# Tiles of u split whole, attention output's weights split a tile ahead, dummy matmuls at the start: one step of a hybrid RG-LRU / attention / PEER block

## The chip, the cores and the metric

One core of one Trainium2 chip runs the whole program. The metric is the device time of one launch in microseconds, the median of several executions. The engines are TensorE (PE, with its weight loads as PEld), VectorE (DVE), ScalarE (ACT), GpSimd (POOL) and SyncE (SP), which here only issues DMAs.

## The reference, cut to what matters

A block over 512 tokens plus 16 meta tokens, width 1024, all float32. A gated recurrent branch and an attention branch are mixed into h. Then comes a product-key expert layer (PEER) over 16384 experts, and a last norm:

```python
n1 = _rmsnorm(h, norm1_g[l])
xr, gr, cq, ckv, kr, g_rnn, g_att = jnp.split(n1 @ w_in[l], IN_SPLITS, axis=-1)
...
y_att = o @ w_attn_out[l]
mixed = jax.nn.sigmoid(g_rnn) * y_rnn + jax.nn.sigmoid(g_att) * y_att
h = h + mixed @ w_out[l]
h = h + _peer(_rmsnorm(h, norm2_g[l]), ...)
...
# _peer, per block of 128 tokens
s1, s2 = q1 @ keys1.T, q2 @ keys2.T          # 8 heads, 128 keys each
t1, i1 = lax.top_k(s1, 16);  t2, i2 = lax.top_k(s2, 16)
ts, sel = lax.top_k(t1 + t2 (all pairs), 16);  idx = the chosen experts
act = jax.nn.gelu(jnp.einsum('chkd,cd->chk', u[idx], xt))
coef = softmax(ts) * act
return jnp.einsum('chk,chkd->cd', coef, v[idx])
```

## The kernel before, in words

Every large product is made of three matmuls of fp32r operands (`mm3`): each operand is split into a high part, a rounding copy made on ACT, and a low part, what is left, made by a subtraction on DVE (`split`, L154 to L156). PE takes high by high, low by high and high by low (L181 to L183). The weights of the dense layers come tile by tile through `wload` (L160 to L173): a tile of 1024 by 128 is loaded as two halves of 128x512 by two DMAs on SP, and each half has its own cast and its own subtraction. The raw halves, the high and the low parts each have a ring of three buffers in the pool "wstream".

The work runs in this order. **Start**: the columns of x and the first weights are loaded, the norm's gain is split into n1h and n1l, squares are taken on ACT (L263) and added on DVE (L265), and PE makes the latents' products (`wckv`) and then the sum of squares `n_ss` over partitions. Then come the projections, the recurrence and the attention. **Mixing** (`mixing`, L672): for each of eight column tiles m, the output weights of attention (`watt`) are split, PE makes `ya`, and the tile is mixed. **Key scores** (`key_scores`, L724): 16 tiles of the query weights `wq`, the scores against the keys, and the two best-eight passes of DVE over each row.

**PEER.** Three of the four blocks of 128 tokens (named 1, 2, 3 in the order of `ORDER`) are computed densely: for each of 128 tiles j of experts, PE makes `a` = u tile times the tokens (24 matmuls of 384 columns), ACT takes its gelu, DVE multiplies it by a gate matrix `gt`, and PE makes `y` = v tile times that (18 matmuls of 512 columns). Block 0 is computed by gathers of its chosen rows of u and v on POOL's queue (`first_by_index` L926, `second_by_index` L935) with multiply-adds on DVE. The gate matrices of the dense blocks are made ahead in a **scatter stage** (`scatter`, L843 to L894): for each group of eight heads' columns DVE builds one-hot matrices `hb` (128x1024, bf16) and `hot` (128x1024, fp32), ACT scales `wj`, PE multiplies them into `sc`, ACT copies `stg`, a DMA stores them to DRAM (`gd`). While that runs, PE makes the first 44 tiles of `a` (`first_ahead`, L830), and DVE also makes the choice of the best pairs (`choose`, L757 to L815: rounds of best-eight, then products over 256 to 1600 columns, L803 to L806). The **dense stage** then runs tile a(j+41) and y(j) in turn.

The tiles of u (`ut`) go through `wload` as well. Up to the dense stage a scheduler sets each engine's order; in the dense stage the order is that of the program. **Tail** (L993 to L1011): for each block of tokens two adds of y on DVE, squares and a square root on ACT, a reciprocal on DVE, and two multiplications (L1010) on DVE, each followed by a DMA on SP.

## Time and profile before

| | before |
|---|---|
| time, median of 3 runs | 1863.86 us (1862.81 to 1864.69) |
| the profiled execution: its own time | 1864.08 us |
| the profiled execution: span from first to last instruction | 1862.3 us, granted clock 0.994 |
| PE busy | 1811.8 us, 97% |
| DVE busy | 1444.0 us, 78% |
| ACT busy | 968.5 us, 52% |
| POOL busy | 355.2 us, 19% |

The span lies 1.8 us below the execution's own time, and the execution 0.2 us above the median of the runs. Busy shares are averages over stages with different limits: the dense stage alone lasts from about 960 to 1853 us.

### The profile page before, as it was taken

How to read it: one execution, taken by the hardware profiler on the slowest of the kernel's cores; microseconds unless marked ns; L12 is line 12 of the kernel's file. 1: busy time of each engine (PE TensorE's matmuls, PEld its weight loads, DVE VectorE, ACT ScalarE, POOL GpSimd, SP SyncE). 2: the span in 40 equal slices, each digit the busy share in tenths (PEclk: the TensorE clock that was granted, in tenths of full speed). 3: DMA queues.
4: the chain of work that ended last, by engine and by line, in shares of the span. 5: the costliest groups of instructions: out<-in, count | busy, mean ns of one | idle time of the engine just before them, and what ended most of it. 6: DMA issues, size and time to landing. Idle time of an engine off the chain costs nothing.

```text
span 1862.3 us, 28323 instructions
## 1 busy us (share of the span) xinstructions
PE 1811.8 (97%) x9731; PEld 1601.3 (86%) x9731; DVE 1444.0 (78%) x3088; ACT 968.5 (52%) x2011; POOL 355.2 (19%) x295
## 2 busy tenths in 40 slices
PE   8999999999899999999999999999999999999997
PEld 7888778877778889998999999999999999997886
DVE  7787677777546999997558788877888878887775
ACT  6778576766333337999953333433333333333343
POOL 0100000000100000000014344434444443543310
PEclk9999999999999999999999999999999999999999
DMA  5333212112743223445589999998998989988764
GB/s 163 96 98 105 74 55 66 57 60 75 237 131 125 80 85 125 177 164 193 191 295 336 324 322 352 318 315 307 321 332 310 322 310 322 333 300 272 266 219 153
DMA packets 181600, 390.32 MB, mean 210 GB/s; under 512 B 16593, under 2 KB 68305, under 8 KB 179921
## 3 DMA queue, kind: packets, MB, share of 16 engines
q1 hardware_dynamic: 141632, 245.97, 39.0%
q0 software_dynamic: 39536, 142.00, 22.1%
q8 instruction: 76, 1.25, 0.3%
q10 hardware_dynamic: 288, 0.56, 0.1%
q14 instruction: 68, 0.55, 0.1%
HBM read 353.44 MB, written 34.08 MB: 208 GB/s over the span
## 4 chain that ended last, share of the span: by engine, by line
PE 30%; issue 16%; POOL 6%; DMA 5%; DVE 4%; ACT 1%; DVEq 0%; POOLq 0%; ACTq 0%
PE y L183 5%; PE y L181 5%; PE y L182 5%; PE a L183 4%; POOL v L915 4%; PE a L181 4%; PE a L182 4%; PE sc L869 4%; DMA v<-in_peer_v_dram,eidx 3%; POOL u L915 2%; DMA u<-in_peer_u_dram,eidx 1%; DVE hot L884 1%; DMA gt<-gd 1%; DMA ut_w<-in_peer_uT_dram 0%; DVE ut_l L156 0%
## 5 line engine op out<-in xcount | busy, mean ns | idle before, releaser
L183 PE MATMUL a<-xdh,ut_l 128*128 128x384 f32 x1024 | 347.4, 339 | 9.2 <-DVE ut_l L156 9.2
L181 PE MATMUL a<-xdh,ut_h 128*128 128x384 f32 x1024 | 348.6, 340 | 1.7 <-ACT ut_h L155 1.4
L182 PE MATMUL a<-xdl,ut_h 128*128 128x384 f32 x1024 | 345.5, 337 | 0.3 <-DVE xdl L156 0.3
L155 ACT CAST ut_h<-ut_w 128x512 fp32r<-128x512 f32 x256 | 157.8, 624 | 327.2 <-DMA ut_w<-in_peer_uT_dram 277.9
L181 PE MATMUL y<-vh,ch 128*128 128x512 f32 x768 | 299.6, 390 | 5.4 <-ACT ch L155 5.4
L183 PE MATMUL y<-vh,cl 128*128 128x512 f32 x768 | 301.6, 393 | 0.0
L182 PE MATMUL y<-vl,ch 128*128 128x512 f32 x768 | 301.0, 392 | 0.0
L915 POOL DMA_INDIRECT u<-in_peer_u_dram,eidx x128 | 161.4, 1261 | 666.3 <-DMA gt<-gd 441.4
L915 POOL DMA_INDIRECT v<-in_peer_v_dram,eidx x128 | 175.4, 1370 | 266.8 <-DVE acc L935 239.7
L156 DVE TENSOR_TENSOR ut_l<-ut_w,ut_h 128x512 fp32r<-128x512 f32 x256 | 169.5, 686 | 54.5 <-ACT ut_h L155 51.3
L183 PEld LDWEIGHTS a<-xdh,ut_l 128*128 128x128 f32 x1024 | 194.1, 190 | 11.4 <-DVE ut_l L156 11.0
L181 PEld LDWEIGHTS a<-xdh,ut_h 128*128 128x128 f32 x1024 | 194.3, 190 | 6.1 <-ACT ut_h L155 2.3
L182 PEld LDWEIGHTS a<-xdl,ut_h 128*128 128x128 f32 x1024 | 194.1, 190 | 3.9 <-DVE xdl L156 0.5
L156 DVE TENSOR_TENSOR vl<-vr,vh 128x1024 fp32r<-128x1024 f32 x128 | 157.6, 1232 | 42.9 <-ACT vh L155 41.9
L155 ACT CAST ch<-gt 128x384 fp32r<-128x384 f32 x128 | 65.7, 513 | 232.4 <-DVE gt L965 227.7
L181 PEld LDWEIGHTS y<-vh,ch 128*128 128x128 f32 x768 | 144.7, 188 | 34.8 <-ACT ch L155 6.5
L935 DVE SCALAR_TENSOR_TENSOR acc<-v,coef,acc 128x1024 f32<-128x1024 f32 x128 | 164.1, 1282 | 10.5 <-DMA v<-in_peer_v_dram,eidx 8.5
L183 PEld LDWEIGHTS y<-vh,cl 128*128 128x128 f32 x768 | 144.4, 188 | 31.1 <-DVE cl L156 0.8
L182 PEld LDWEIGHTS y<-vl,ch 128*128 128x128 f32 x768 | 144.5, 188 | 28.5
L926 DVE SCALAR_TENSOR_TENSOR jk<-u,xn 128x1024 bf16<-128x1024 f32 x128 | 156.6, 1223 | 13.7 <-DMA u<-in_peer_u_dram,eidx 11.3
L155 ACT CAST vh<-vr 128x1024 fp32r<-128x1024 f32 x128 | 133.8, 1045 | 32.5 <-PE y L183 28.5
L156 DVE TENSOR_TENSOR cl<-gt,ch 128x384 fp32r<-128x384 f32 x128 | 71.5, 559 | 81.8 <-ACT ch L155 81.8
(348 smaller groups left out, 3470.2 us busy)
## 6 DMA issues: line engine op xcount, KB each, us to landing
ut_w<-in_peer_uT_dram SPq DMA_DIRECT2D x256, 256.0 KB, 6.1
vr<-in_peer_v_dram SPq DMA_DIRECT2D x128, 512.0 KB, 6.7
...
```

What stands on the lines that cost most here:

```text
L155: A.copy(dst_hi, src)
L156: V.tensor_sub(dst_lo, src, r32(dst_hi))
L181: TE.matmul(o, lh, rh, start=first, stop=False)
L182: TE.matmul(o, lh, rl, start=False, stop=False)
L183: TE.matmul(o, ll, rh, start=False, stop=last)
L869: TE.matmul(o[:, u * P:(u + 1) * P], hot[:, h + u, :], wj[:, h + u, :], start=True, stop=True)
L884: V.tensor_tensor(hot, iota.unsqueeze(1).to_broadcast([P, SG, P]), it[:, t0:t0 + SG].unsqueeze(2).to_broadcast([P, SG, P]), op=OP.is_equal)
L915: G.indirect_dma_start(out=t, out_offset=None, in_=src, in_offset=bass.IndirectOffsetOnAxis(ap=eidx[:, s:s + 1], axis=0))
L926: V.scalar_tensor_tensor(jk, t, 1.0, xn2, op0=OP.mult, op1=OP.mult, accum_out=coef[:, s:s + 1])
L935: V.scalar_tensor_tensor(acc, t, coef[:, s:s + 1], acc, op0=OP.mult, op1=OP.add)
```

## The change: whole tiles of u, weights of mixing ahead, dummy matmuls, and a tail on three engines

1. **u.** From tile 1 on, a tile of u is loaded by one DMA of 128x1024, and has one cast and one subtraction of 128x1024 (`uparts`). Tile 1 goes through the ring of v (`vr`, `vh`, `vl`), earlier than before; the others have rings of two whole tiles in a pool "ustream", which is opened where the weights' pool is closed, after the key scores. The pool "choice" moves to the other side of the memory.
2. **Mixing.** The load and split of watt for tile m+1 stand before the mixing of tile m.
3. **Start.** Ten matmuls of a 128x128 matrix of ones stand ahead of all others; ACT runs in program order there, which puts the squares behind the casts; the loads are written into the same loop.
4. **Tail.** For the first dense block (`fo1`) ACT scales by the reciprocal and POOL multiplies by the gain, instead of DVE.

```diff
+WARM = 10
-WB, RB, GB, VB, XB = 3, 3, 4, 3, 1
+WB, RB, GB, VB = 3, 3, 4, 3
...
-    wp = pool(ctx, "wstream")
+    wpx = ExitStack()
+    ctx.enter_context(wpx)
+    wp = pool(wpx, "wstream")
...
-        i = k * m
-        hi, lo = w[i // 512]
-        return hi[:, i % 512:i % 512 + m], lo[:, i % 512:i % 512 + m]
+        i, n = k * m, w[0][0].shape[-1]
+        hi, lo = w[i // n]
+        return hi[:, i % n:i % n + m], lo[:, i % n:i % n + m]
...
-    for k in range(NK):
-        nc.sync.dma_start(h0[k], hT[:, k * T:(k + 1) * T])
-        if k == 0:
-            w0 = wload(win[3], D, "wckv0")
     V.memset(onesP, 1.0)
     V.memset(eps_t, EPS)
-    A.activation(one_t, onesP[:, 0:1], AF.Identity)
-    for k in range(NK):
-        gk = vec[:, V_G1 + k:V_G1 + k + 1]
-        A.activation(n1h[:, k, :], h0[k], AF.Identity, scale=gk)
-        V.scalar_tensor_tensor(n1l[:, k, :], h0[k], gk, r32(n1h)[:, k, :], op0=OP.mult, op1=OP.subtract)
-    lat = [now(proj_tile(3 + k, True, f"wckv{k}", w=None if k else w0)) for k in range(2)]
-    sq = two(("cv", "aa"), "sq")
-    for k in range(NK):
-        A.activation(sq[k], h0[k], AF.Square)
-        if k:
-            V.tensor_add(sq[0], sq[0], sq[k])
+    warm = mm1("warm")
+    for _ in range(WARM):
+        TE.matmul(warm[:, :P], onesP, onesP, start=True, stop=True)
+    with in_order(tc, mybir.EngineType.Activation):
+        A.activation(one_t, onesP[:, 0:1], AF.Identity)
+        for k in range(NK):
+            nc.sync.dma_start(h0[k], hT[:, k * T:(k + 1) * T])
+            gk = vec[:, V_G1 + k:V_G1 + k + 1]
+            A.activation(n1h[:, k, :], h0[k], AF.Identity, scale=gk)
+            V.scalar_tensor_tensor(n1l[:, k, :], h0[k], gk, r32(n1h)[:, k, :], op0=OP.mult, op1=OP.subtract)
+            if k == 0:
+                w0 = wload(win[3], D, "wckv0")
+        lat = [now(proj_tile(3 + k, True, f"wckv{k}", w=None if k else w0)) for k in range(2)]
+        sq = two(("cv", "aa"), "sq")
+        for k in range(NK):
+            A.activation(sq[k], h0[k], AF.Square)
+            if k:
+                V.tensor_add(sq[0], sq[0], sq[k])
...
-            w = wload(peer_uT[j], D, f"ut{j}")
+            w = uload(j) if j else wload(peer_uT[j], D, f"ut{j}")
...
+        nw = wload(watt[0], D, "watt0")
         for m in range(NK):
-            w = wload(watt[m], D, f"watt{m}")
+            w = nw
...
             o = mm2(f"ya{m}")
             for k in range(NK):
                 mm3(o, *wsl(w, k), *ot[k], k == 0, k == NK - 1)
+            if m + 1 < NK:
+                nw = wload(watt[m + 1], D, f"watt{m + 1}")
...
-    po_ = pool(postx, "choice")
+    po_ = pool(postx, "choice", "right")
...
+    def uparts(j, pl, tags, bufs):
+
+        raw, hi, lo = (pl.tile([P, D], dt, tag=t, bufs=n, name=f"ut{j}_{t}")
+                       for t, n, dt in zip(tags, bufs, (F32, F32R, F32R)))
+        nc.sync.dma_start(raw, peer_uT[j])
+        split(hi, lo, raw)
+        return [(hi, lo)]
+
+    def uload(j):
+        return uparts(j, up, ("uw", "uh", "ul"), (2, 2, 2))
...
+            if m == 2 * PH - 1:
+                nextw[1] = uparts(1, vp, ("vr", "vh", "vl"), (VB, 2, 2))
             if m:
                 scores(m - 1, last)
             last = q2
-            if m == 2 * PH - 1:
-                nextw[1] = wload(peer_uT[1], D, "ut1")
...
-            w = nextw.pop(j, None) or wload(peer_uT[j], D, f"ut{j}")
+            w = nextw.pop(j, None) or uload(j)
             if j + 1 <= LAG - LT:
-                nextw[j + 1] = wload(peer_uT[j + 1], D, f"ut{j + 1}")
+                nextw[j + 1] = uload(j + 1)
...
     interleave((key_scores(), 17), (ga[0], na_[0]))
+    wpx.close()
+    up = pool(dx, "ustream")
...
-    wn[:] = 0, XB, vq
...
-        w = wload(peer_uT[j + LAG], D, f"ut{j + LAG}") if j + LAG < NJ else None
+        w = uload(j + LAG) if j + LAG < NJ else None
...
-            V.scalar_tensor_tensor(fo[:, cs], y[:, cs], st[:, 2:3], gfb[:, cs], op0=OP.mult, op1=OP.mult)
+            if i == 0:
+                A.activation(fo[:, cs], y[:, cs], AF.Copy, scale=st[:, 2:3])
+                G.tensor_mul(fo[:, cs], fo[:, cs], gfb[:, cs])
+            else:
+                V.scalar_tensor_tensor(fo[:, cs], y[:, cs], st[:, 2:3], gfb[:, cs], op0=OP.mult, op1=OP.mult)
```

The scheduler orders the engines anew after this. Three places of the new order follow; names carry the program's numbers, and line numbers of the changed kernel are its own (there L158 and L159 are the cast and the subtraction of a split).

DVE in the scatter stage, before, around the low part of tile 24 of u (`ut24_l`); `hb1`, `hot1` are the one-hot matrices of block 1, and `work0`, `oh0`, `efx0` the last steps of the choice for block 0:

```order
L803 TENSOR_TENSOR work0_9438<-sf0_10079,cand_pos_6197 128x640
L805 TENSOR_TENSOR oh0_1_10161<-work0_9438,cx0_9441 128x32x20
L884 TENSOR_TENSOR hot1_80_9118<-iota_73,it1_8523 128x1024
L879 TENSOR_TENSOR hb1_88_9147<-iota4_6199,blk1_8521 128x1024
L156 TENSOR_TENSOR ut24_l0_9068<-ut24_w0_9065,ut24_h0_9067 128x512
L156 TENSOR_TENSOR ut24_l512_9074<-ut24_w512_9071,ut24_h512_9073 128x512
L884 TENSOR_TENSOR hot1_88_9149<-iota_73,it1_8523 128x1024
L806 TENSOR_REDUCE efx0_80<-oh0_1_10161 128x8x4
L879 TENSOR_TENSOR hb1_96_9216<-iota4_6199,blk1_8521 128x1024
L803 TENSOR_TENSOR work0_9438<-sf0_10079,cand_pos_6197 128x1120
L805 TENSOR_TENSOR oh0_2_10244<-work0_9438,cx0_9441 128x32x35
L806 TENSOR_REDUCE efx0_80<-oh0_2_10244 128x8x4
```

The same place of the changed kernel:

```order
L826 TENSOR_REDUCE efx0_80<-oh0_1_9960 128x8x4
L899 TENSOR_TENSOR hb1_72_8929<-iota4_6210,blk1_8434 128x1024
L823 TENSOR_TENSOR work0_9291<-sf0_9884,cand_pos_6208 128x1120
L825 TENSOR_TENSOR oh0_2_10037<-work0_9291,cx0_9294 128x32x35
L904 TENSOR_TENSOR hot1_72_8931<-iota_73,it1_8436 128x1024
L826 TENSOR_REDUCE efx0_80<-oh0_2_10037 128x8x4
L899 TENSOR_TENSOR hb1_80_8987<-iota4_6210,blk1_8434 128x1024
L823 TENSOR_TENSOR work0_9291<-sf0_9884,cand_pos_6208 128x1600
L825 TENSOR_TENSOR oh0_3_10111<-work0_9291,cx0_9294 128x1600
L904 TENSOR_TENSOR hot1_80_8989<-iota_73,it1_8436 128x1024
L159 TENSOR_TENSOR ut24_ul_8944<-ut24_uw_8942,ut24_uh_8943 128x1024
L899 TENSOR_TENSOR hb1_88_9018<-iota4_6210,blk1_8434 128x1024
```

The steps of the choice over 1120 and most of those over 1600 columns, which followed tile 24's part, now stand ahead of it.

SP's queue at the beginning of mixing, before; `wga` are the gates' results that are stored, `wo` the weights of the product after mixing:

```order
L166 DMA watt0_w0_5379<-in_watt_dram 128x512
L166 DMA watt0_w512_5385<-in_watt_dram 128x512
L352 DMA sad_60<-wga5_s_5241 128x512
L640 DMA wo_w0_0_5424<-in_wout_dram 128x512
L352 DMA sad_60<-wga6_s_5304 128x512
L166 DMA watt1_w0_5430<-in_watt_dram 128x512
L166 DMA watt1_w512_5436<-in_watt_dram 128x512
```

And in the changed kernel:

```order
L169 DMA watt0_w0_5390<-in_watt_dram 128x512
L169 DMA watt0_w512_5396<-in_watt_dram 128x512
L358 DMA sad_60<-wga5_s_5252 128x512
L169 DMA watt1_w0_5430<-in_watt_dram 128x512
L358 DMA sad_60<-wga6_s_5315 128x512
L169 DMA watt1_w512_5436<-in_watt_dram 128x512
L646 DMA wo_w0_0_5447<-in_wout_dram 128x512
```

The first half of watt1 has taken the place of wo's first load, ahead of the store of wga6.

ACT at the end of the changed kernel (before, the row L1032 is not there and the others are the same):

```order
L1026 ACTIVATE fo1_17909,fst1_17908<-yt1_17891 128x512 x2
L1026 ACTIVATE fo2_17924,fst2_17923<-yt2_17893 128x512 x2
L1028 ACTIVATE fst1_17908<-fst1_17908,eps_t_79 128x1
L1026 ACTIVATE fo3_17937,fst3_17936<-yt3_17895 128x512 x2
L1032 ACTIVATE fo1_17909<-yt1_17891,fst1_17908 128x512 x2
L1028 ACTIVATE fst2_17923<-fst2_17923,eps_t_79 128x1
L1028 ACTIVATE fst3_17936<-fst3_17936,eps_t_79 128x1
```

The two scalings of block 1 (L1032) stand ahead of the square roots (L1028) of blocks 2 and 3.

## Rows read from the trace of the kernel before

**Rows 1.** The table by stretches; the columns stand in its first line.

```profile
core 0: us, PE busy (x) PEld busy (x) DVE busy (x) ACT busy (x) POOL busy (x), PEclk, DMA share, GB/s
5.82:11.90 6.08, 6.08 (x24) 5.55 (x25) 5.93 (x10) 5.91 (x11) 0.00 (x0) 1.00 1.04 360
11.91:20.70 8.79, 8.79 (x74) 8.79 (x74) 8.65 (x25) 7.15 (x12) 0.00 (x0) 1.00 0.53 156
671.00:860.00 189.00, 176.83 (x1135) 172.05 (x1134) 184.23 (x660) 153.06 (x401) 0.00 (x0) 0.96 0.42 152
860.00:959.20 99.20, 97.95 (x670) 96.97 (x668) 52.34 (x69) 88.31 (x230) 1.58 (x2) 1.00 0.58 203
1000.00:1680.00 680.00, 680.00 (x3439) 618.95 (x3438) 555.65 (x750) 247.66 (x410) 286.74 (x222) 1.00 0.92 320
688.80:694.60 5.80, 5.72 (x18) 5.72 (x19) 5.67 (x44) 1.00 (x2) 0.00 (x0) 0.50 0.43 136
```

**Rows 2.** Timeline, 13 to 21 us, DVE and PE.

```profile
14.03 1.28 DVE L156 TENSOR_TENSOR wckv_l<-wckv_w,wckv_h 128x512 fp32r<-128x512 f32 x2
...
17.71 0.70 DVE L265 TENSOR_TENSOR sq_cv<-sq_cv,sq_aa 128x528 f32<-128x528 f32 x1
...
18.52 0.17 DVE L333 TENSOR_TENSOR cl<-cl 128x8 f32<-128x8 f32 x1
...
20.68 1.05 PE L208 MATMUL n_ss<-sq_cv,onesP 128*128 128x264 f32 x4
```

**Rows 3.** Timeline, 467 to 502 us, SP, PE and ACT.

```profile
467.00 3.54 SPq L166 DMA_DIRECT2D watt_w<-in_watt_dram  x2
...
471.40 0.39 PE L228 MATMUL wga_ps<-n1h,wga_l 128*128 128x512 f32 x1
...
472.99 0.62 ACT L155 CAST watt_h<-watt_w 128x512 fp32r<-128x512 f32 x1 [3.52 <-DMA watt_w<-in_watt_dram]
...
473.66 0.50 PE L181 MATMUL ya<-oth,watt_h 128*128 128x512 f32 x1 [1.86 <-ACT watt_h L155]
...
501.18 0.50 PE L181 MATMUL ya<-oth,watt_h 128*128 128x512 f32 x1 [2.70 <-ACT watt_h L155]
```

**Rows 4.** The page, part 5: groups; mean ns of one, idle before it, releaser.

```profile
L183 PE MATMUL a<-xdh,ut_l 128*128 128x384 f32 x1024 | 347.4, 339 | 9.2 <-DVE ut_l L156 9.2
...
L156 DVE TENSOR_TENSOR ut_l<-ut_w,ut_h 128x512 fp32r<-128x512 f32 x256 | 169.5, 686 | 54.5 <-ACT ut_h L155 51.3
...
L156 DVE TENSOR_TENSOR vl<-vr,vh 128x1024 fp32r<-128x1024 f32 x128 | 157.6, 1232 | 42.9 <-ACT vh L155 41.9
```

**Rows 5.** Timeline, 688 to 850 us, DVE and PE.

```profile
688.88 0.69 PE L183 MATMUL a<-xdh,ut_l 128*128 128x384 f32 x1 [3.52 <-DVE ut_l L156]
...
840.44 1.29 DVE L156 TENSOR_TENSOR ut_l<-ut_w,ut_h 128x512 fp32r<-128x512 f32 x2
...
841.18 0.58 PE L183 MATMUL a<-xdh,ut_l 128*128 128x384 f32 x1 [0.65 <-DVE ut_l L156]
```

**Rows 6.** Groups of DVE by line and shape, 671 to 860 us.

```profile
L879 DVE TENSOR_TENSOR hb<-iota,blk 128x1024 bf16<-128x1024 bf16 x32 | 21.9, 684 | 0.6 <-ACT wj L888 0.6
L805 DVE TENSOR_TENSOR oh<-work,cx 128x1600 f32<-128x1600 bf16 x4 | 7.3, 1818 | 0.0
...
L806 DVE TENSOR_REDUCE efx<-oh 128x32 f32<-128x1120 f32 x4 | 5.3, 1316 | 0.1
...
L803 DVE TENSOR_TENSOR work<-sf,cand_pos 128x1600 bf16<-128x1600 bf16 x4 | 3.9, 985 | 0.0
...
L806 DVE TENSOR_REDUCE efx<-oh 128x32 f32<-128x640 f32 x4 | 3.3, 816 | 0.1
...
L803 DVE TENSOR_TENSOR work<-sf,cand_pos 128x1120 bf16<-128x1120 bf16 x4 | 2.9, 734 | 0.0
```

**Rows 7.** Timeline, 1854 to 1858 us, ACT and DVE.

```profile
1854.69 0.28 ACT L1007 ACTIVATE fst<-fst,eps_t 128x1 f32<-128x1 f32 x1
...
1855.61 1.41 DVE L1010 SCALAR_TENSOR_TENSOR fo<-yt,fst,gfb 128x512 f32<-128x512 f32 x2
```

## Prediction, made before the changed kernel was run

> **What bounds the kernel now.** I read the table by stretches first. In the dense stage PE is busy for all of it: 680.00 of 680.00 us between 1000 and 1680, with DVE at 556 and ACT at 248 [rows 1]. Whatever shortens DVE's or ACT's work there is worth nothing in time. PE's busy time of 1811.8 in a span of 1862.3 (the table of times) leaves 50 us in all, so the change has to earn its time in the places where PE waits. The groups of the page name one such wait, 9.2 us in all for the low parts of u [rows 4], and the table shows where it lies: from 671 to 860 DVE is busy for 184 of 189 us and PE for 177 [rows 1]. There DVE's queue sets the pace, and its order decides when each tile's low part is ready. Before that, PE waits at two places of mixing, 1.86 and 2.70 us for a cast of watt [rows 3], and at the beginning. At the end nothing covers the tail.
>
> **Whole tiles of u.** Two subtractions of 128x512 stand at a mean of 686 ns each [rows 4], as a pair they take 1.29 us [rows 5], 0.08 less than twice the mean; one of 128x1024, as v has them, takes 1.23 [rows 4]. So a tile saves 0.06 us of DVE as the queue runs. For 87 tiles in the dense stage that would be 5 us of DVE's time, but PE is what runs there, so I take 0. If that cover were gone, 5 us would be all there is. The bytes are the same, the raw ring is two whole tiles instead of one and a half, and no row of before has PE waiting for them.
>
> What moves is the order in the scatter stage. Two places count.
>
> First, tile 2. Before, DVE makes its second half just before 688.88, behind the last key scores, and PE waits 3.52 us for it [rows 5]. After, the order has the whole subtraction at the same place. Tile 1's parts and tile 2's first half no longer stand ahead, but most of that room is lost: DVE waits there for scores that ACT copies out, and the copies come when PE has made them. With two casts fewer ahead of the last copies on ACT I take 0.3 us. PE then has the whole tile to make after the part is there, not half of it, but DVE sets the pace from there on and PE catches up.
>
> Second, tile 24. Before, its pair starts at 840.44 and PE waits 0.65 us for it at 841.18 [rows 5]. After that, PE waits only 1.3 us until the dense stage begins: 97.95 busy of 99.20 [rows 1]. So that is the last place at which DVE's queue binds, and a change there reaches the end. In the changed order the steps of the last block's choice that came behind tile 24 now stand ahead of it: sums over 1120 and 640 columns (1.32 and 0.82), products over 1600 and 1120 (1.82, and 1.32 taken as the sum of that width), comparisons over the same (0.99 and 0.73), together 7.0 us by their means [rows 6]. Three short steps come ahead as well and one one-hot hb (0.68) falls behind; I set these against each other. That is eight instructions more, and with 0.08 off for each, as in the pair, 6.4. Whole tiles give back 23 x 0.06, and the half of tile 1 that has gone elsewhere 0.6: 2.0. Tile 24 comes 6.4 - 2.0 = 4.4 us later against the scores, 0.3 of which tile 2's place gives back: 4.1. What is late next is PE: its work behind tile 24 is the same, and it can use the 1.3 us in which it waited before. So the dense stage begins 4.1 - 1.3 = **2.8 us later**. Bounds: if DVE's whole queue up to the dense stage decides and not tile 24, the stage ends earlier by what that queue saves, about 26 tiles at 0.06 and two halves of tile 1 that went elsewhere at 0.6: 2.8 us. Upwards, 4.1 with nothing absorbed, and a second stretch at the lower clock: behind the wait at 688.88, from 688.8 to 694.6, PE made 18 matmuls in 5.80 us at a granted clock of 0.50 [rows 1], 0.32 each, and at the full clock would have needed half of it; I take 1.7 for a stretch a little longer than half as long. So -2.8 to +5.8.
>
> **Mixing.** The load of watt1 is issued at 467.00, its cast runs at 472.99 after 3.52 us for the DMA, and PE restarts at 473.66 [rows 3]. Now the load's first half stands ahead of a store and of wo's load, some 5 us earlier, so the DMA is off the path. The cast then needs a buffer that the last gate product on PE gives back; that product starts at 471.40 and takes 0.39 [rows 3]. Cast at 471.85 instead of 472.99: **1.1 us**. The second wait (2.70 at 501.18) comes from a cast queued on ACT behind wo's cast, whose DMA is late; in the new order wo's load of one tile less stands at the same place. I leave it at 0. Bounds: 0 to 3.8, if both go (1.1 + 2.7).
>
> **Start.** [...] But PE's queue then reaches `n_ss`, the sum of squares, which needs DVE's seven adds. Before, three of them stood ahead of wckv's last low part and four behind, the last started at 17.71, and n_ss at 20.68 [rows 2], held by PE's own work. After, the squares come behind all casts, and all seven adds behind the low parts. Without three adds (0.62 each as the queue runs, 0.70 less the overlap) the last low part, a pair that began at 14.03 and took 1.28, ends at 13.4; seven adds are 4.3, and about a dozen short steps of 0.17 to 0.2 between them 2.3 [rows 2]: 20.05, and n_ss follows. So n_ss starts at about 20.15 instead of 20.68: **0.5 us**, between 0 and 1.5, as the short steps count. [...]
>
> **Tail.** The scalings of block 1 on ACT stand ahead of the square roots of blocks 2 and 3. The root of block 2 ran at 1854.69 [rows 7]; two scalings of about 0.52 each move it to 1855.74, the root itself takes 0.28, and I give the reciprocal and the hand-overs as much, so the multiplication, which ran at 1855.61 [rows 7] behind block 1's, would run at about 1856.3. DVE's two multiplications less do not help, since it is the root that it waits for. Block 3's pair follows as much later: **0.7 us slower**, between 0.3 and 1.3.
>
> **Sum.** -0.5 - 1.1 + 2.8 + 0.7 = +1.9. The profiled execution's 1864.08 becomes 1866.0; its 0.2 above the median taken off, **1865.8**.
>
> **Rivals.**
> A, faster: tile 24 does not bind, since ACT or PE hold DVE up there anyway, and the shorter queue counts; both waits of mixing go. -0.5 - 3.8 - 2.8 + 0.7 = -6.4: 1857.5. For it: DVE's total work does fall. Against it: DVE idles for 5 us only in those 189 [rows 1].
> B, slower: DVE's new order around tile 24 counts in full. PE waits over 4 us there, and the lower clock that follows such a wait (it did at 688.88) costs another 1.7: 5.8 in place of 2.8, so +4.9 and 1868.8. It decides from +4.6 in this stage, where the sum passes the 3.7 below. For it: the tile's part is 4.4 us further down a queue that is never idle for long. Against it: part of the work ahead may run in gaps that before stood behind.
> C, the tail is held up: POOL's multiplication of fo1 has no row in this trace, and SP sends fo1's result ahead of the others'. If DVE's multiplications for blocks 2 and 3 had to wait for POOL, and POOL takes no less than DVE does for its pair (1.41 [rows 7]), 1.4 comes on top: +3.3, 1867.2. [...]
> D, the change does little: the gains of start and mixing are swallowed by later waits and the order turns out neutral, 1864.
>
> **Chances.** This kernel's runs agree within 0.1%, and 0.2%, 3.7 us, is what can be told from no change. The forecast 0.32, C 0.07 and D 0.08 lie within it: same 0.47. A has 0.25 (faster), B 0.28 (slower). The range reaches from near A to beyond B: 1858 to 1870.5. The forecast's own: 1863.5 to 1867.5.
>
> **What would show it.** Right: n_ss at about 20.15; PE's restart in mixing at 472.5; a wait of PE for tile 24's low part of some 4 us, and the first y about 3 us later against the key scores; the dense stage with PE busy throughout, as before; the last multiplications some 0.7 us later behind the last matmul. Wrong: no wait at tile 24, or a new one for a cast or a load of u in the scatter stage (the rings' sizes), or gathers that come at another time and so shift the few waits of PE after the last tile of u, which I have left at no change.

## The result, and the profile after

The changed kernel took 1873.7 us (median of five runs, 1870.83 to 1875.54). The kernel before took 1862.81 on the same chip (1859.85 to 1864.69). The ratio is 1.0060, 95% interval 1.0046 to 1.0074: slower by 0.6%, above the predicted range. The profiled execution took 1872.85 with a span of 1871.1 us, 8.8 more than before.

The table by stretches, as [rows 1]:

```profile
core 0: us, PE busy (x) PEld busy (x) DVE busy (x) ACT busy (x) POOL busy (x), PEclk, DMA share, GB/s
671.00:860.00 189.00, 172.23 (x1103) 167.18 (x1101) 180.02 (x628) 147.26 (x363) 6.02 (x4) 0.95 0.42 149
860.00:959.20 99.20, 98.13 (x673) 97.63 (x672) 51.36 (x51) 87.81 (x224) 0.00 (x0) 1.00 0.58 215
704.70:711.50 6.80, 6.05 (x19) 6.05 (x20) 5.89 (x6) 0.00 (x0) 0.00 (x0) 0.50 0.47 157
960.00:975.00 15.00, 7.69 (x31) 6.26 (x30) 3.86 (x5) 2.46 (x5) 0.00 (x0) 0.77 0.85 251
1000.00:1680.00 680.00, 680.00 (x3441) 619.22 (x3440) 549.97 (x672) 245.65 (x328) 292.18 (x222) 1.00 0.92 322
```

The dense stage reads as before: PE busy for all 680.00 us, DVE with 5.7 us less work. The loss lies ahead of it. From 671 to 860 PE is busy for 172.2 us instead of 176.8, and from 960 to 975 for about half of the time. Both kernels have a stretch at a granted clock of 0.50 around the wait for tile 2 (before from 687.7 to 694.5, changed from 684.2 to 691.0, 6.8 us each); the changed kernel has a second one, of 6.8 us from 704.7 to 711.5, where before it was 1.00.

To see where each microsecond goes, I put milestones of the two traces side by side: the start of tile k's gelu on ACT, the first y, the last a, the last matmul and the end of the span. All are counted from ACT's copy of the last scores but one (675.54 here, 677.39 before). That copy itself comes 1.9 us earlier. Tile 2's gelu runs at 694.06, 18.5 behind the copy; before it ran at 692.49, 15.1 behind: 3.4 later. In the same way:

| us later than before, from the copy | tile 2 | tile 5 | tile 12 | tile 20 | tile 24 | tile 40 | first y | last a | last matmul | end |
|---|---|---|---|---|---|---|---|---|---|---|
| after | 3.4 | 7.5 | 7.6 | 6.4 | 7.3 | 6.4 | 11.9 | 12.9 | 7.7 | 10.7 |

So the span's +8.8 is: -1.9 up to the scores, +7.5 by tile 5 and nothing more up to tile 40 (-1.1), +5.5 before the first y, +1.0 in the dense stage, -5.2 behind the last tile of u, +3.0 in the tail. The rows of each, in order:

**Start and mixing**, timeline of PE, as [rows 2, 3]:

```profile
20.30 0.94 PE L211 MATMUL n_ss<-sq_cv,onesP 128*128 128x264 f32 x3 [1.30 <-DVE sq_cv L271]
...
471.68 0.50 PE L184 MATMUL ya<-oth,watt_h 128*128 128x512 f32 x1 [0.52 <-ACT watt_h L158]
...
497.75 0.50 PE L184 MATMUL ya<-oth,watt_h 128*128 128x512 f32 x1 [0.90 <-ACT watt_h L158]
```

The sum of squares starts at 20.30 (20.68 before), mixing restarts at 471.68 (473.66), and the second stop is 0.90 us instead of 2.70. That makes 3.4 us by 497.75 (501.18 before), of which 1.6 are given back to other short waits before the scores.

**Tiles 2 and 5**, timeline of ACT, DVE and PE, as [rows 5]:

```profile
675.54 0.59 ACT L767 COPY scs<-sc 128x512 f32<-128x512 f32 x1 [0.29 <-PE sc L765]
676.15 0.49 DVE L771 MAX8 tv<-scs 128x8 f32<-128x128 f32 x2 [1.57 <-ACT scs L767]
...
686.30 1.22 DVE L159 TENSOR_TENSOR ut_ul<-ut_uw,ut_uh 128x1024 fp32r<-128x1024 f32 x1
...
704.17 2.36 DVE L159 TENSOR_TENSOR ut_ul<-ut_uw,ut_uh 128x1024 fp32r<-128x1024 f32 x2
...
687.57 0.69 PE L186 MATMUL a<-xdh,ut_ul 128*128 128x384 f32 x1 [5.75 <-DVE ut_ul L159]
...
705.45 0.69 PE L186 MATMUL a<-xdh,ut_ul 128*128 128x384 f32 x1 [1.68 <-DVE ut_ul L159]
```

DVE is busy with the last best-eight passes (`tv`) and a few short steps from 676.15 to 686.3. The low part of tile 2 comes behind them, and PE waits 5.75 us for it. Before, PE had made half of that tile by then and waited 3.52 us.

Tile 5's part is late as well. It is the first of the two at 704.17, 28.6 us behind the copy; before, its halves ran at 697.92 and 699.92, 20.5 and 22.5 behind. Ahead of it, DVE now makes the choice's steps over 256, 640 and most of those over 1120 columns (698.6 to 704.2), which before came behind it. PE waits 1.68 us for the part at 705.45, behind two shorter stops of 0.60 and 0.72 at 701.82 and 703.16, and the second stretch at 0.50 lies there. To weigh the two places, here is the stretch from the copy to 24 us behind it, and the one from 24 to 36, first of the kernel before, then of the changed one:

```profile
677.39:701.39 24.00, 20.48 (x105) 20.12 (x105) 22.36 (x157) 6.74 (x13) 0.00 (x0) 0.86 0.28 88
701.39:713.39 12.00, 12.00 (x71) 12.00 (x70) 11.90 (x31) 7.61 (x12) 0.00 (x0) 1.00 0.37 113
675.54:699.54 24.00, 18.02 (x96) 17.38 (x96) 23.28 (x164) 7.08 (x10) 0.00 (x0) 0.86 0.20 62
699.54:711.54 12.00, 9.00 (x33) 8.05 (x32) 10.98 (x15) 3.56 (x5) 0.00 (x0) 0.72 0.29 97
```

By tile 2, PE has made 96 matmuls instead of 105; at 12.00 us for 71 that is some 1.5 us of work. Around tile 5 it makes 33 instead of 71, some 6.4 us. Part of this comes back later.

From tile 5's gelu to tile 20's, PE then stands idle for about as long as before, 5.9 us instead of 6.5. But the largest of its waits is another one; before, then changed:

```profile
PE a L183 <- DVE ut_l L156: 4.0, 2, 3.1
PE sc L889 <- ACT wj L908: 5.0, 3, 2.1
```

The waits for low parts have shrunk to 0.4 us, those for ACT's scalings `wj` have grown from 0.6.

**Tile 24**, where the prediction saw the loss, timeline of DVE and PE, as [rows 5]:

```profile
845.13 1.22 DVE L159 TENSOR_TENSOR ut_ul<-ut_uw,ut_uh 128x1024 fp32r<-128x1024 f32 x1
...
845.36 0.68 PE L889 MATMUL sc<-wj,hot 128*128 128x128 f32 x4 [0.99 <-ACT wj L908]
846.40 0.44 PE L186 MATMUL a<-xdh,ut_ul 128*128 128x384 f32 x1 [0.36 <-DVE ut_ul L159]
```

PE waits 0.36 us for the low part, and 0.99 for the scalings `wj` ahead of it. The part comes 6.5 us later against the copy than before (169.6 us behind it instead of 163.1), but PE itself is late by about as much (tile 20's gelu by 6.4), so it finds the part nearly ready. Between tiles 20 and 24 the kernel loses 0.9 us, and by tile 40 it has made that good.

**The first y**, timeline of SP, DVE and PE:

```profile
952.70 0.33 SPq L892 DMA_DIRECT2D gd<-stg  x1
...
957.92 0.50 SPq L981 DMA_DIRECT2D vr<-in_peer_v_dram  x1
960.69 0.33 SPq L969 DMA_DIRECT2D acc<-h2d  x1
961.07 6.75 SPq L979 DMA_DIRECT2D gt<-gd  x6
...
969.99 0.56 DVE L986 TENSOR_TENSOR gt<-gt,act 128x384 f32<-128x384 f32 x1 [12.09 <-DMA gt<-gd]
...
971.15 0.79 PE L184 MATMUL y<-vh,ch 128*128 128x512 f32 x1 [6.31 <-ACT ch L158]
```

The same loads in the kernel before, and SP's one wait from 940 to 975 us that ended with the landing of a store of `gd`, before and changed:

```profile
950.87 5.33 SPq L958 DMA_DIRECT2D gt<-gd  x3
SPq L958 <- DMA gd<-stg: 2.2, 1, 2.2
SPq L969 <- DMA gd<-stg: 2.2, 1, 2.2
```

The first loads of a gate tile `gt` are issued at 961.07, behind loads of v (`vr`) and of `acc`, and 8.4 us behind the last store of `gd` (952.70). DVE has idled 12.09 us when it can multiply, and PE waits 6.31. From that store to the first y it is 18.5 us. Before it was 12.8 (948.29 to 961.08, a wait of 1.79). There the first two of the three loads went out (950.87, 952.15) while the last store was under way; only the third waited until it had landed, and went out at 955.83, 7.5 us behind it. Now SP waits for that landing at `acc`, ahead of all three, and the third goes out at 962.74, 10.0 us behind the store; DVE can multiply 7.3 us after that, before 4.1.

**Behind the last tile of u**, PE's waits from 1000 us on (us in total, times, longest), first of the kernel before, then of the changed one:

```profile
PE y L181 <- ACT ch L155: 3.6, 2, 2.8
```

```profile
PE y L184 <- ACT ch L158: 0.8, 1, 0.8
```

A stop of 2.8 us at 1686.53 is gone, and with it the lower clock there: from 1680 to 1700 PE's granted clock was 0.91 before and is 1.00 now.

**The tail**, timeline of PE, ACT, POOL and DVE, as [rows 7]:

```profile
1858.72 0.39 PE L186 MATMUL y<-vh,cl 128*128 128x512 f32 x1
...
1860.55 1.32 ACT L1032 ACTIVATE fo<-yt,fst 128x512 f32<-128x512 f32 x2
...
1861.33 2.93 POOL L1033 TENSOR_TENSOR fo<-fo,gfb 128x512 f32<-128x512 f32 x2 [69.50 <-ACT fo L1032]
1861.77 0.46 ACT L1028 ACTIVATE fst<-fst,eps_t 128x1 f32<-128x1 f32 x2
...
1862.28 2.53 DVE L1035 SCALAR_TENSOR_TENSOR fo<-yt,fst,gfb 128x512 f32<-128x512 f32 x2
```

The last matmul starts at 1858.72 (1852.86 before). Block 2's multiplications start 3.56 us behind it instead of 2.75, and the pair takes 2.53 us instead of 1.41, with POOL's pair beside it. The last store is issued 7.64 us behind the last matmul instead of 5.71.

### The profile page after: what moved, and what is told of

The parts are those of the page before. It is cut to its first block, busy times and chain, and to the rows that moved or that the text cites. A ratio compares the mean times of both kernels' runs of the same rounds, so it can differ in the third digit from the quotient of the medians.

```text
span 1871.1 us, 27656 instructions
## 1 busy us (share of the span) xinstructions
PE 1815.2 (97%) x9751; PEld 1604.0 (86%) x9751; DVE 1433.5 (77%) x2959; ACT 963.2 (51%) x1886; POOL 369.3 (20%) x297
## 4 chain that ended last, share of the span: by engine, by line
PE 79%; DVE 11%; ACT 5%; DMA 3%; issue 1%; SPq 0%; ACTq 0%; DVEq 0%
PE y L185 9%; PE y L186 9%; PE y L184 9%; PE a L186 8%; PE a L185 8%; PE a L184 8%; PE wga_ps L231 2%; PE q L184 2%; PE sc L889 2%; PE q L185 2%; PE wgr_ps L231 2%; PE q L186 2%; PE wgn_ps L231 2%; DMA wo_w<-in_wout_dram 1%; DVE hot L904 1%
## 5 line engine op out<-in xcount | busy, mean ns | idle before, releaser
L186 PE MATMUL a<-xdh,ut_ul 128*128 128x384 f32 x1008 | 341.5, 339 | 8.5 <-DVE ut_ul L159 8.5
L184 PE MATMUL a<-xdh,ut_uh 128*128 128x384 f32 x1008 | 343.7, 341 | 3.3 <-ACT act L840 1.9
L185 PE MATMUL a<-xdl,ut_uh 128*128 128x384 f32 x1008 | 340.2, 338 | 0.0
L937 POOL DMA_INDIRECT u<-in_peer_u_dram,eidx x128 | 172.3, 1346 | 664.0 <-ACT stg L890 339.1
L158 ACT CAST vh<-vr 128x1024 fp32r<-128x1024 f32 x128 | 134.9, 1054 | 268.2 <-issue 228.0
L159 DVE TENSOR_TENSOR vl<-vr,vh 128x1024 fp32r<-128x1024 f32 x128 | 156.8, 1225 | 88.6 <-ACT vh L158 79.6
L186 PEld LDWEIGHTS a<-xdh,ut_ul 128*128 128x128 f32 x1008 | 191.1, 190 | 9.9 <-DVE ut_ul L159 9.8
L184 PEld LDWEIGHTS a<-xdh,ut_uh 128*128 128x128 f32 x1008 | 191.5, 190 | 8.4 <-ACT act L840 2.9
L185 PEld LDWEIGHTS a<-xdl,ut_uh 128*128 128x128 f32 x1008 | 191.3, 190 | 3.3
L158 ACT CAST ch<-gt 128x384 fp32r<-128x384 f32 x128 | 65.6, 513 | 238.6 <-DVE gt L986 235.6
L158 ACT CAST ut_uh<-ut_uw 128x1024 fp32r<-128x1024 f32 x126 | 132.6, 1054 | 91.6 <-PE a L185 77.0
L159 DVE TENSOR_TENSOR ut_ul<-ut_uw,ut_uh 128x1024 fp32r<-128x1024 f32 x126 | 153.5, 1219 | 24.4 <-ACT ut_uh L158 23.6
L159 DVE TENSOR_TENSOR cl<-gt,ch 128x384 fp32r<-128x384 f32 x128 | 71.6, 559 | 81.1 <-ACT ch L158 81.1
```

The source lines that it names most:

```text
L158: A.copy(dst_hi, src)
L159: V.tensor_sub(dst_lo, src, r32(dst_hi))
L184: TE.matmul(o, lh, rh, start=first, stop=False)
L185: TE.matmul(o, lh, rl, start=False, stop=False)
L186: TE.matmul(o, ll, rh, start=False, stop=last)
L937: G.indirect_dma_start(out=t, out_offset=None, in_=src, in_offset=bass.IndirectOffsetOnAxis(ap=eidx[:, s:s + 1], axis=0))
```

## The experiments

The last column of the table is the ratio to runs of the kernel before on the same chip. The columns ahead of it are the milestones above, from one profile of each kernel. How far they repeat is seen in e3 and e4 below, which leave u and the pools as before: up to the first y, their milestones stay within 1.1 us of before's.

| us later than before | tile 2 | tile 5 | tile 20 | tile 24 | tile 40 | first y | last matmul | end | ratio [95%] |
|---|---|---|---|---|---|---|---|---|---|
| e1 tail back | 4.5 | 4.7 | 2.6 | 3.6 | 4.4 | 10.1 | 6.2 | 6.1 | 1.0041 [1.0028, 1.0054] |
| e2 u only | 4.3 | 6.3 | 5.7 | 6.5 | 7.1 | 12.1 | 8.7 | 8.6 | 1.0046 [1.0033, 1.0059] |
| e5 gate first | 4.7 | 4.7 | 3.7 | 4.4 | 4.6 | 7.0 | 3.5 | 3.5 | 1.0027 [1.0016, 1.0038] |
| e6 halves | 2.5 | -0.4 | -0.8 | 0.4 | -1.7 | 4.8 | 0.5 | 0.5 | 1.0009 [0.9998, 1.0021] |
| e7 DVE's order as before | 3.9 | 1.0 | 1.9 | 3.1 | 2.7 | 8.0 | 4.5 | 4.4 | 1.0014 [1.0000, 1.0029] |
| e8 before, DVE's order as after | 2.8 | 8.0 | 17.8 | 32.1 | 32.4 | 30.8 | 33.0 | 33.1 | 1.0164 [1.0144, 1.0184] |
| e10 halves, gate first | 3.6 | 0.7 | -1.0 | 0.2 | -1.3 | 1.8 | -1.5 | -1.5 | 0.9985 [0.9975, 0.9995] |
| e11 halves, DVE as before | 2.5 | 1.5 | 2.4 | 9.3 | 5.8 | 11.1 | 7.9 | 7.8 | 1.0033 [1.0021, 1.0045] |
| e12 tile 24 first | 3.4 | 7.4 | 6.3 | 9.1 | 10.2 | 15.7 | 13.0 | 12.9 | 1.0049 [1.0035, 1.0063] |
| e13 three high parts | 4.2 | 5.5 | 12.2 | 18.2 | 20.4 | 26.9 | 53.3 | 58.5 | 1.0293 [1.0258, 1.0328] |
| e14 halves, both queues | 1.3 | 0.2 | 0.2 | 0.2 | 1.7 | 6.7 | 3.1 | 3.0 | 1.0008 [0.9993, 1.0022] |
| e15 whole, both queues | 2.7 | 0.1 | 5.0 | 4.8 | 9.8 | 15.0 | 11.3 | 11.3 | 1.0051 [1.0031, 1.0071] |
| e18 tile 2 early | -5.8 | -1.7 | -1.6 | -1.0 | -1.1 | 4.2 | 1.1 | 1.1 | 1.0000 [0.9986, 1.0014] |
| e19 tile 2 early, gate first | -5.8 | -2.6 | -1.0 | -0.4 | -0.5 | 0.8 | -2.8 | -2.8 | 0.9989 [0.9975, 1.0004] |

### Which part of the change costs: e1 to e4

e1 is the changed kernel with the tail of before:

```diff
-            if i == 0:
-                A.activation(fo[:, cs], y[:, cs], AF.Copy, scale=st[:, 2:3])
-                G.tensor_mul(fo[:, cs], fo[:, cs], gfb[:, cs])
-            else:
-                V.scalar_tensor_tensor(fo[:, cs], y[:, cs], st[:, 2:3], gfb[:, cs], op0=OP.mult, op1=OP.mult)
+            V.scalar_tensor_tensor(fo[:, cs], y[:, cs], st[:, 2:3], gfb[:, cs], op0=OP.mult, op1=OP.mult)
```

> The changed kernel with the tail of before, all else and every other row of the order the same. Theory: between the last matmul and the end the changed kernel's profile needs about 3 us more than that of before (12.0 against 9.0), all of it from ACT's scalings ahead of two square roots and from POOL's multiplication; so this one lies 3 us under the changed kernel, about 6 us over before, and the first pair of multiplications for block 2 takes 1.4 us again where it took 2.5. Rival: the end is set by the last DMA and the program's closing, and the tail's engines matter little: under 1 us.

e2 is the changed kernel with start, mixing and tail of before, so that only u and the pools are changed:

> Before with the whole tiles of u and the moved pools alone (start, mixing and tail as before). From the key scores on its order is that of the changed kernel. Theory: the loss sits in two places, DVE's order in the scatter stage (+6 us by the first tiles to the last one made ahead) and the first y, which waits for the gate matrix's load (+5 to 6 us), against some 4 us that come back when the last tiles of u are through: in all +7 to +9 us over before. Rival: the scatter stage suffers because key scores end 2 us earlier and the loads meet other traffic, so that without start and mixing the loss is under 4 us.

e3 is the kernel before with the changed start and mixing:

> Before with the new start and the new mixing alone; from the key scores on the order is that of before. Theory: the gain of 1.9 us that the changed kernel has at the key scores is kept to the end: -1.5 to -2.5 us. Rival: DVE's queue in the scatter stage or the first y's wait swallows it: -0.5 to +0.5.

e4 is the kernel before with the changed tail:

> Before with the new tail alone. Theory: +2.5 to +3.5 us; block 2's square root some 1.2 us later behind the last matmul, and its pair of multiplications 2.5 us long instead of 1.4, beside POOL's of 1.5 each. Rival, the prediction's own term: only the roots' delay counts, +0.7 (0.3 to 1.3).

e3 gave 0.9993 [0.9974, 1.0011] and e4 1.0009 [0.9998, 1.0020], e1 and e2 both over 1.004. So u and the pools alone make the loss. Start and mixing bring the scores 3.1 us earlier in e3's profile; its times spread from 1856 to 1871, so the ratio says little. The tail, from the last matmul's start to the end, takes 12.1 us in e4 and 9.4 in e1; it was 9.4 before and is 12.4 after. That is +3 us with either kernel around it.

### The tail without POOL: e9

```diff
-                G.tensor_mul(fo[:, cs], fo[:, cs], gfb[:, cs])
+                V.tensor_mul(fo[:, cs], fo[:, cs], gfb[:, cs])
```

> The changed kernel, with DVE in POOL's place: ACT scales fo1 as there, and DVE multiplies it by the gain. Theory (two parts of the tail's 3 us: the later roots, and DVE standing still while POOL reads): block 2's root stays 1.2 us later behind the last matmul than in before, its pair of multiplications takes 1.4 us again instead of 2.5, and the time from the last matmul to the end is 0.8 to 1.8 us over before's 9.4, instead of 3.0. Rival: POOL has nothing to do with it and the tail stays at 12.0 to 12.4.

The tail took 10.4 us. Timeline of DVE:

```profile
1860.61 1.30 DVE L1033 TENSOR_TENSOR fo<-fo,gfb 128x512 f32<-128x512 f32 x2 [0.45 <-ACT fo L1032]
...
1862.02 2.74 DVE L1035 SCALAR_TENSOR_TENSOR fo<-yt,fst,gfb 128x512 f32<-128x512 f32 x4
```

The first row is block 1's pair, the second has blocks 2 and 3 together: 2.74 us for four multiplications, 1.37 a pair, with POOL idle. So of the 3.0 us about 1.0 stays without POOL: the roots are as late as in the changed kernel (block 2's 3.05 us behind the last matmul, before 1.83), and block 1's pair is on DVE again. The other 2.0 go with POOL. DVE's longer pair shows in 0.9 of them (the last store is issued 6.74 us behind the last matmul, with POOL 7.64); the rest lies behind that issue, 4.7 us to the end instead of 3.7, and why was not tried. The whole kernel gave 1.0041 [1.0022, 1.0059] (after: 1.0060).

### The first y: e5 and e10

e5 is e1 with the first gate tile's loads (their names are kept in `g0`) ahead of `acc` and of the fourth load of v:

```diff
-    nc.sync.dma_start(acc, h2d[0:P, :])
...
+    def behind(first):
+        tc.add_manual_dep(nc.cur_bb.bb.instructions[-1], first, mybir.DependencyInfo(
+            mybir.DependencyClass.NoSync, mybir.DependencyReason.DATA), reason="queue")
...
         nc.sync.dma_start(vr, peer_v[j * P:(j + 1) * P, :])
+        if j == 3:
+            behind(g0[-1])
...
         nxt = stage(0)
+        nc.sync.dma_start(acc, h2d[0:P, :])
+        behind(g0[-1])
```

> The kernel of e1 (the changed one with the tail of before), with the loads of the first gate matrix ahead of the loads of vr3 and of the gathers' sum on SP's queue; DVE's order is unchanged. Theory: the first y waited 6.5 us because those two stood ahead and were themselves waiting; it now starts 4 to 5.5 us earlier than in e1, and the whole time falls by as much, to about 1.5 us over before. Rival 1: the load waits for the last store of the gate matrices in any case, and the first y gains under 1.5 us. Rival 2: what is gained at the first y is given back by the waits of PE behind the last tile of u.

e10 is e6 (below) with that, and with `acc` and the gain `gfb` loaded behind the load of v's tile 8:

> The kernel of e6 (whole loads of u into the new rings, cast and subtracted in halves, tail of before), with the first gate matrix loaded first and the loads of the gathers' sum and of the gain moved behind vr8. Theory: the stretch from the gelu of tile 40 to the first y falls from 12.6 to 7 to 9 us and all else stays, so it is about 4 us under e6, 1859 to 1860, faster than before by 0.15 to 0.3%. Rival: the loads of the gate matrix have to wait for the last store and come no earlier: within 1 us of e6.

From tile 40 to the first y e5 loses 2.4 us where e1 lost 5.7, and e10 3.1 where e6 lost 6.5. So 3.3 us of the 5.5 are the place of these loads in SP's queue. (The first y of e5 comes 3.1 us earlier than e1's, where 4 to 5.5 were expected.) In both the first load itself now waits for the landing of the last store (3.2 us in e5, 4.1 in e10), and the third goes out 9.7 and 9.3 us behind that store, before the change 7.5. e10 is the one kernel here that is faster than the kernel before beyond its interval.

### The scatter stage: size, order, rings (e6 to e8, e11)

e6 is e1 with the cast and the subtraction in halves, the loads and the buffers whole:

```diff
-        split(hi, lo, raw)
+        for c in (slice(0, 512), slice(512, D)):
+            split(hi[:, c], lo[:, c], raw[:, c])
```

> The kernel of e1, with each tile of u loaded by one DMA into the new rings as there, but cast and subtracted in two halves of 128x512. Theory (the order that the scheduler makes is what costs, not the size of a piece): the scatter stage, from the low part of tile 2 to the gelu of tile 40, stays 3 to 7 us longer than before's or moves with the new order, while the dense stage is the same within 1 us. Rival (a tile that is ready only as a whole is what costs in the scatter stage): it returns to before's length, within 1.5 us.

e7 is e1 with DVE's instructions of the scatter stage in the order of the kernel before, and e8 the kernel before in the order of e1. Both chain the instructions by a table:

```diff
+    for a, b in zip(DVEQ, DVEQ[1:]):
+        tc.add_manual_dep(q[b], q[a].name, mybir.DependencyInfo(
+            mybir.DependencyClass.NoSync, mybir.DependencyReason.DATA), reason="queue")
```

> The kernel of e1, with DVE's queue in the scatter stage (490 instructions) in the order that before had, a whole subtraction standing where the second half stood. Theory: DVE's order is the cause of the longer scatter stage; from tile 2's low part to the gelu of tile 40 it takes 4 to 6 us less than in e1 and is within 1.5 us of before's 266.8. Rival: with whole tiles it is the ring or the later readiness of a whole tile that holds PE, and the stage stays within 1.5 us of e1's.

> Before, with DVE's queue in the scatter stage in the order of the changed kernel, both halves of a tile where the whole subtraction stands; rings, loads and pools as before. Theory: the stage from tile 2's low part to the gelu of tile 40 grows by 4 to 7 us over before's 266.8. Rival, as in e7: it stays within 1.5 us of before's.

e11 is e6 with DVE's order of before, by the same means:

> The kernel of e6 with DVE's queue in the scatter stage in before's order, 528 instructions: against e7 only the size of u's pieces differs (and the order of other engines as the scheduler makes it), against before the loads, rings and pools. Theory now: order and size of piece each cost about half; from tile 2's low part to the gelu of tile 40 it takes 266 to 267.5 us, as in before, 2 to 3 us less than e7's 269.6. Rival: the new rings and pools cost those 2.7 us, and it takes 269 or more.

e6 alone loses nothing by tile 40 (-1.7), although PE waits 5.18 us at tile 2 there too. e7 gets back the loss at tile 5 (1.0 instead of 4.7) and loses 1.7 behind it; by tile 40 it is 1.7 us better than e1, not the 4 to 6 expected. The stretch from 24 to 36 us behind the copy, e1 first, then e7:

```profile
699.41:711.41 12.00, 9.78 (x55) 9.14 (x54) 11.93 (x16) 5.08 (x7) 0.00 (x0) 1.00 0.29 97
698.20:710.20 12.00, 11.85 (x69) 11.53 (x68) 11.48 (x35) 5.57 (x8) 0.00 (x0) 1.00 0.32 93
```

Before there were 71 matmuls in it, and 71 in e6. In e7 PE still waits 5.73 us at tile 2, but tile 5's part starts 23.2 us behind the copy instead of 28.6, and its cast on ACT, which the scheduler placed anew, 21.8 instead of 25.2. So the loss around tile 5 comes with the place that the new order gives the tile, and what tile 2 costs is left: 2.7 us at tile 40. e8 loses 32 us, far more than the whole change does and more than I had reckoned with. e11 was to be at least as good as e6 if DVE's order of before were good by itself; it loses 6.9 us between tiles 20 and 24. An order of DVE forced on other sizes or buffers makes losses of its own (e8, e11), so what e7 has lost by tile 40 may be partly of that kind.

### Tile 24 and the ring: e12 and e13

In e12, only tile 24's low part is moved, eight instructions up in DVE's order of e1 (a table, as above), where the kernel before had it:

> As e1 (the change with the old tail), but in DVE's order of the scatter stage the low part of tile 24 alone stands eight instructions earlier, ahead of the choice's steps over 1120 and 1600 columns, as before the change. Theory of the prediction (tile 24's place in DVE's queue binds): the stage from tile 2's low part to the gelu of tile 40 falls from e1's 271.3 us by about 3 to 4.4, to 267 to 268.3, and the time with it. Rival (the loss is made all along the stage, where ACT's casts of whole tiles wait for one of two buffers with the scalings wj behind them): one tile moved leaves the stage at 270 to 272.

e13 is e1 with a third buffer for high parts, and DVE's order held as in e1:

```diff
-WB, RB, GB, VB = 3, 3, 4, 3
+WB, RB, GB, VB = 3, 3, 4, 2
...
-        return uparts(j, up, ("uw", "uh", "ul"), (2, 2, 2))
+        return uparts(j, up, ("uw", "uh", "ul"), (2, 3, 2))
```

> As e1 with a ring of three whole high parts of u instead of two (the raw ring of v gives up one of its three for the room), DVE's order in the scatter stage held as in e1. Theory of the rings (casts wait for PE to free a high part, and the scalings wj behind them on ACT are late): ACT's waits of ut_uh for PE fall from about 19 us to under 10, PE's waits of sc for wj from 6.4 to about 2 to 3, the stage from 271.3 to about 267. Theory of the queue (DVE's order alone): PE's waits stay near 17 and the stage within 1 us of 271.3. The dense stage may wait for loads of v and is not compared.

Neither theory held. e12, timeline of DVE and ACT:

```profile
842.96 1.23 DVE L184 TENSOR_TENSOR ut_ul<-ut_uw,ut_uh 128x1024 fp32r<-128x1024 f32 x1 [7.45 <-ACT ut_uh L183]
...
836.17 2.48 ACT L933 ACTIVATE wj<-hb,gt 128x128 f32<-128x128 bf16 x8
...
839.50 2.50 ACT L933 ACTIVATE wj<-hb,gt 128x128 f32<-128x128 bf16 x8
841.89 1.04 ACT L183 CAST ut_uh<-ut_uw 128x1024 fp32r<-128x1024 f32 x1
```

DVE stands 7.45 us for the cast, which is behind two groups of scalings (`wj`) in ACT's queue, and the part comes at 842.96, not earlier than in e1 (841.30). The kernel loses 3.9 us between tiles 20 and 40 that the changed kernel doesn't lose. In e13, ACT's waits of the casts from 671 to 870 (us in total, times, longest), e13 first, then e1:

```profile
ACT ut_uh L183 <- DMA ut_uw<-in_peer_uT_dram: 18.2, 6, 9.9
...
ACT ut_uh L183 <- PE a L210: 1.8, 1, 1.8
```

```profile
ACT ut_uh L158 <- PE a L185: 23.9, 4, 13.0
```

The waits for PE went, as expected, from 23.9 to 1.8 us, but the same casts now wait 18.2 for loads, and tile 40 comes 16 us later than in e1.

### Both queues as before: e14 and e15

e14 is e6, e15 is e1, with the orders of DVE and ACT both held as before:

> As e6 (whole loads and whole buffers, cast and subtraction in halves), with both DVE's and ACT's order in the scatter stage held as in the kernel before; e11 held DVE's alone and took 273.4 us. Theory that a queue's order costs where the other queue's order does not fit it: with both as before the stage returns to 266 to 268 us (before 266.9). Rival, that the new buffers cost by themselves, since a whole one comes free only when PE is through with both halves: the stage stays at 270 or more, and ACT's waits of the casts for PE stay above 20 us.

> As e7 (whole tiles, DVE's order as before, 269.6 us) with ACT's order in the scatter stage held as before too. Theory of the two queues: 267 to 269. Rival, that whole casts at the head of ACT's queue hold up the scalings wj behind them whatever the order: 270 or more, with PE's waits of sc for wj at 4 us or more.

e14's PE waits from 671 to 870:

```profile
PE a L241 <- DVE ut_ul L214: 10.1, 5, 4.4
PE sc L945 <- ACT wj L964: 2.0, 2, 1.5
PE a L239 <- ACT ut_uh L213: 1.2, 1, 1.2
```

With halves and both orders as before, the new buffers cost next to nothing: 0.2 us from tile 3 to tile 28, 1.7 at tile 40. Counted from tile 2's low part, the stage takes 269.3 us by its first half and 267.9 by its second, from which the 266.8 of before are counted; 266 to 268 were expected. With whole tiles and the same orders (e15), the loss is 9.8 at tile 40, worse than e7. PE waits for both parts there:

```profile
PE a L237 <- DVE ut_ul L210: 8.5, 10, 4.8
PE a L235 <- ACT ut_uh L209: 4.7, 5, 1.2
```

That is 13.2 us, against 11.3 in e14. So orders that fit halves don't fit whole tiles, and for e15 my theory failed. Its rival expected waits of 4 us or more for `wj`, and those are 0.8; around tile 5 e15 loses nothing either (0.1).

### Tile 2 alone: e18 and e19

e18 is e1 with tile 2 taken through v's ring beside tile 1, early:

```diff
-                nextw[1] = uparts(1, vp, ("vr", "vh", "vl"), (VB, 2, 2))
+                for j in (1, 2):
+                    nextw[j] = uparts(j, vp, ("vr", "vh", "vl"), (VB, 2, 2))
...
-            if j + 1 <= LAG - LT:
+            if j + 1 <= LAG - LT and j + 1 not in nextw:
```

> As e1, but tile 2 of u goes through the ring of v's parts beside tile 1, and is split long before the last key scores instead of behind DVE's last best-eight passes. Theory (the scatter stage's loss is made at tiles 2 to 5, where PE stands 5.75 us for a whole low part of tile 2 with all of its 24 matmuls still to make, and is never made good): the wait of 5.75 us falls to 1 to 3 us, at tile 3 now; the gelu of tile 5 comes 3 to 5 us earlier against the scores than in e1, and so does that of tile 40. Rival (the steps from tile 5 on set the end of the stage, PE catches up whatever happens before): the gelu of tile 40 stays within 1.5 us of e1's.

e19 is e18 with e10's order of loads:

> As e18, with the loads of the first gate tile ahead of the other loads and those of acc and of the gain gf behind the load of v's tile 8, as in e10. If both effects add: the first y 3 to 3.5 us earlier than in e18, and with the gain of e18 a time below that of the kernel before by 1 to 4 us; if one eats the other, no better than e10 (0.9985 of before).

e18's PE waits 2.05 us, for tile 3:

```profile
688.56 0.44 PE L186 MATMUL a<-xdh,ut_ul 128*128 128x384 f32 x1 [2.05 <-DVE ut_ul L159]
```

The loss of the scatter stage is gone: -1.7 at tile 5, -1.1 at tile 40, 5.5 less than e1. The kernel is as fast as the one before. The scheduler also moved the low parts of tiles 4 to 11 up among the steps of the choice, so this run doesn't part tile 2 from tile 5, as e7 does; both belong to the stretch between the scores and tile 5. In e19 the two effects add. SP and PE:

```profile
947.36 0.33 SPq L893 DMA_DIRECT2D gd<-stg  x1
...
954.88 2.47 SPq L982 DMA_DIRECT2D gt<-gd  x3
...
961.47 0.79 PE L184 MATMUL y<-vh,ch 128*128 128x512 f32 x1 [3.76 <-ACT ch L158]
```

From the last store to the first y it is 14.1 us (18.1 in e18), and the time is about e10's, though the interval still holds no change.

## Why the prediction was wrong

**Start and mixing** held in the number, -1.6 forecast and 1.9 us at the scores, and only partly in the terms. The start is right (n_ss at 20.30, 20.15 forecast). That PE would be through with its own products by then, so that n_ss could follow the adds, is a premise that no row of before shows; the changed kernel shows it. PE's first 24 matmuls took 6.08 us before, 0.253 each, and the 74 behind them 0.119 each [rows 1]. Behind the dummies the first 24 took 4.60 us (5.39 to 9.99), stops of 0.18 and 0.42 among them, and the 74 behind them 0.122 each; the granted clock stands at 1.00 in all four. The products end at 19.00 (20.68 before), and PE waits 1.30 us for the last add. Mixing's restart is right as well: its wait fell by 1.3 us (1.1 forecast). The second wait, left at 0, gave 1.8, and other waits took 1.6 back: that these two nearly cancel is luck.

**Whole tiles in the dense stage** held: PE is busy throughout, and DVE's 5.7 us less are worth nothing.

**The scatter stage** failed. The forecast was +2.8 from tile 24, and 0.3 gained at tile 2. Measured are +6.4 at tile 40 and nothing left of tile 24. The step that failed is "Two places count", with the sentence on the first of them: "PE then has the whole tile to make after the part is there, not half of it, but DVE sets the pace from there on and PE catches up." PE doesn't catch up. It waits 5.75 us at tile 2 instead of 3.52, falls some 1.5 to 2.5 us of matmuls behind (96 in the changed kernel and 90 in e1, where before made 105), and in e7, where nothing else is lost up to tile 5, 2.7 us are still there at tile 40. And there is a third place, tile 5, which the prediction put at nothing without a reason. There the choice's steps now stand ahead of the tile's part, just as it had seen them ahead of tile 24's. PE falls back by another 6.4 us of matmuls in the changed kernel and 2.7 in e1; e7, e15 and e6, with other orders or halves, lose next to nothing there. So the mechanism of the forecast (a part further down DVE's queue) and of rival B (a stretch at a granted clock of 0.50 beside a wait, here the 6.8 us from 704.7) was right, and its place was wrong. In the changed kernel, e2 and e12 tile 5 is 1.6 to 2.8 us later than in e1. The changed kernel has its stretch at 0.50 there; e1, with the same order, stopped 1.04 us at 703.51 and 1.17 at 705.30 and stayed at 1.00 (704 to 711). So this part comes and goes. e18 shows that the loss at tile 40 goes when both places are mended in whole tiles, and e6 that halves do it too. What PE waits for behind tile 5 changed from low parts to `wj`; whether those are late because of whole casts in ACT's queue was not parted.

Tile 24's part came 6.5 us later, more than the 4.4 of the forecast, and cost nothing that lasted, because PE was late by as much already. Rival A had it right that tile 24 does not bind, though it drew a gain from it. Moved up, the part would not have come sooner: its cast stood behind `wj` on ACT (e12).

**The first y** had no term. The prediction counted the waits up to tile 40 and took what follows as unchanged. It cost 5.5 us, 3.3 of them by the order of SP's loads (e5, e10). The rest, 2.2, can be read from SP's rows: with the new pools the first load of the first gate tile is issued 7.5 us (e19) to 8.7 us (e1) behind the last store of `gd`, when that store has landed (7.5 us after its issue in before's profile), before the change 2.6, so the third load, which waited for the landing in any case, goes out some 2 us later than before (9.3 to 9.7 us behind the store in e5, e10 and e19; before 7.5). That it is the new place of the buffers which makes the first two wait as well is inferred, not shown. e19 loses only 1.3: its first y starts some 4.5 us behind its third load, before 5.3 (955.83 to 961.08).

**Behind the last tile of u** the forecast was no change, with a shift there named among the signs of being wrong, and the changed kernel gains 5.2 us in this profile. In e3 and e4, with the loads of before, last a to last matmul takes 174.6 and 174.0 us, in before's profile 177.6, in the kernels with the new loads 172.5 to 173.0 (e13, with fewer buffers for v, apart). So the gain is between 1.5 and 5, as the run before happens to fall. Why the wait is gone was not tried.

**The tail** was mis-sized: +0.7 forecast, +3.0 measured. ACT's two scalings took 1.32 us, not twice 0.52, a figure for which the prediction had no row, and the roots came 1.2 later; 1.0 of the 3.0 stays without POOL (e9). Rival C, held at 0.07, was right that POOL's pair costs time beyond the roots' delay, 2.0 us (e9) instead of its 1.4: DVE's pair takes 2.53 us beside POOL's and 1.41 without. What makes it longer no row shows.

By the prediction's terms, then: -1.6 became -1.9, +2.8 became +6.4, 0 became +5.5 at the first y, 0 became +1.0 and -5.2 in and behind the dense stage, +0.7 became +3.0. The two terms that were left at nothing, +5.5 and -5.2, nearly cancel in this profile, again by luck. The prediction also took the runs to agree within 0.1%; those of the kernel before that stand beside the experiments spread from 1857 to 1873 us, so its 3.7 us for what can be told was fine enough for medians of many runs, not for single ones.
